# One 128x64 scan state for all heads: narrow state products, row-tiled inter products, one update per block, in a two-layer hybrid mixer

## The chip, the cores and the metric

The kernel runs on one core of one Trainium2 chip. The metric is the device time of one execution in microseconds; the time before is the median of three runs.

## The reference

Two layers act on 1024 latent tokens and 256 context tokens of width 1024. In each layer one input projection feeds three head groups: neighbourhood attention (8 heads), gated linear attention (GLA, 4 heads with keys of 32 and values of 64) and HGRN2 (4 heads with keys and values of 64). GLA and HGRN2 are scans in both directions, first over the context and then over the latents:

```python
def step(state, xs):
    q_i, k_i, v_i, d_i = xs
    o_i = jnp.einsum('bhcd,bhdv->bhcv', q_i, state)
    state = d_i[..., None] * state + jnp.einsum('bhcd,bhcv->bhdv', k_i, v_i)
    return state, o_i
```

`state` is a matrix of keys by values for each head. The output of a chunk is the inter part `o_i`, that reads the state, plus an intra part from the chunk's own tokens. The groups are gated, joined, and projected back with a residual.

## The kernel before

Activations lie with features on the 128 partitions and the 1280 tokens along the free axis, in SBUF buffers of 128x1280 fp32 (`big`, 34 of them). The dense products split an fp32 operand into a high and a low fp32r part and make three matmuls of it (`proj`, L306 to L308, PSUM tile pj); scans and attention multiply in plain fp32.

`scan_run` handles one scan: GLA with `nh=4` heads of `dk=32` keys (`hp = npair = 2` pairs of heads; names that end in g), HGRN2 with two heads of 64 keys at a time (`hp = npair = 1`; names that end in h). Per layer it runs once for GLA and twice for HGRN2, six times in all. The 128 partitions of keys hold all heads of a run, `dk` each. Tokens go in ten blocks of 128, two to a step, with steps 0 to 5 (step 5 has no new block pair) and then a backward loop `k = 2..5`. In a step:

- `prep` (of the next step) makes the decayed keys and queries on GpSimd, ScalarE and VectorE.
- `diag` (tile l, L598), `level` 0 to 2 (tile lv, L639) and `add_levels` (L662) build the intra matrix A of the two blocks. l and lv come from the PSUM pool `pss` (two buffers of two banks).
- `turn` (ktp, L670) transposes the decayed keys of the step before; `states` multiplies them with the values (pu, L682) and updates the forward state. pu and ktp come from `pst` (two buffers of one bank).
- `outs` makes the outputs of the step before: inter products with the state (L698) and intra products with A (L704) into po, which ScalarE copies out (L711).

The backward direction keeps its transposed keys in `ktb`: `back_states` (pub, L721) and `back_outs` (pi, L734, added to the output by VectorE in L742) run in step 5 and in the backward loop. In layer 1 the context blocks need no output.

The state of a run is a block-diagonal 128 x (64 nh) matrix: head h has its rows `h*dk` and its columns `64*h`, the rest is zero. So the state product of a block is one 128x128 product per pair of heads, whose off-diagonal part is thrown away, and `state_step` updates it head by head (L526 for the first block, L528 else: old state times decay plus product), nh VectorE instructions a block. The inter product contracts all 128 rows, against zeros for the other heads: 128 rows by 64 columns a head in `outs`, 128 by 128 a pair in `back_outs`. The forward states rotate through three places in zk, zz_ and ab[0], the backward ones through four in zk, which is cleared again in step 5 (L765).

TensorE and SyncE run in the order in which the program is written; the instructions of the other engines are ordered by a planner's simulated times, and PSUM and SBUF buffers are handed out by it too. Between the parts of a scan stand calls `fill(ns)`: each puts so many nanoseconds' worth of dense projections of later stages into TensorE's order, counted from a table and not from a clock. Wherever a tile of matmul operands is smaller than 128 rows or columns, several such matmuls use different parts of the array.

Of the kernel before, what the change touches and what calls it, by code (L numbers as in the profile page):

```python
# [12 lines left out]
F32 = mybir.dt.float32  # L13
# [6 lines left out]
P = 128  # L20
# [42 lines left out]
def hybrid_kernel(ctx: ExitStack, tc: tile.TileContext, a: dict, out: bass.AP):  # L63
# [424 lines left out]
    def scan_run(l, tag, nh, q, ks, G, dec, gs, vts, vgs, oTs, nxt=()):  # L488
# [5 lines left out]
        sw_ = npair * P  # L494
# [5 lines left out]
        nc.gpsimd.memset(zk, 0.0)  # L500
        nc.gpsimd.memset(zz_, 0.0)
        nc.gpsimd.memset(ab[0][:, 1024:], 0.0)
# [5 lines left out]
        spare = (zk, zz_, ab[0]) if hp == 2 else (zz_, zz_[:, P:], ab[0])  # L508
        Sf = [t[:, 1024:1024 + sw_] for t in spare]
        Sb = [zk[:, sw_ * i:sw_ * i + sw_] for i in range(4)]  # L510
# [165 lines left out]
        def states(e):  # L676
            pu = pst.tile([P, 512], F32, tag="t1", name="pu")
            js = [j for j in range(2) if 2 * e["step"] + j < 9]
            for j in js:
                for pr in range(npair):  # L680
                    c = j * sw_ + pr * P
                    nc.tensor.matmul(pu[:, c:c + P], e["kt"][:, j], vts[pr][:, 2 * e["step"] + j, :], start=True, stop=True)  # L682
            for j in js:
                s = 2 * e["step"] + j
                state_step(0, Sf[s % 3], Sf[(s + 1) % 3], s, s == 0, pu, j * sw_)

        def outs(e, pool, tg):
            if not e["intra"]:
                return
            po = pool.tile([P, 512] if tg == "t1" else [P, 1024], F32, tag=tg, name="po")  # L690
            col = lambda pr, j: slice(256 * pr + P * j, 256 * pr + P * j + P)
            for j in range(2):
                s = 2 * e["step"] + j
                A = e["A"][0] if hp == 1 else e["A"][j]
                for pr in range(npair):
                    for hb in range(2):
                        if s > 0:
# [5 lines left out]
                    for hb in range(2):  # L703
                        nc.tensor.matmul(  # L704
                            po[hb * 64:hb * 64 + 64, col(pr, j)], vts[pr][:, s, hb * 64:hb * 64 + 64],
                            A[:, 2 * hb + j if hp == 1 else 2 * pr + hb, :], start=(s == 0), stop=True,
                            skip_group_check=True,
                        )
            c0 = 256 * e["step"]
            for pr in range(npair):  # L710
                nc.scalar.copy(oTs[pr][:, c0:c0 + 256], po[:, 256 * pr:256 * pr + 256])  # L711
# [3 lines left out]
        def back_states(k):  # L715
            pu = pst.tile([P, 512], F32, tag="t1", name="pub")
            ns = [n for n in (2 * k, 2 * k + 1) if n < 9]
            for i, n in enumerate(ns):
                for pr in range(npair):
                    c = i * sw_ + pr * P  # L720
                    nc.tensor.matmul(pu[:, c:c + P], ktb[:, order[n], :], vts[pr][:, order[n], :], start=True, stop=True)  # L721
            for i, n in enumerate(ns):
                state_step(1, Sb[n % 4], Sb[(n + 1) % 4], order[n], n == 0, pu, i * sw_)

        def back_outs(k):
# [4 lines left out]
            for i, n in enumerate(ns):  # L730
                s = order[n]
                for pr in range(npair):
                    c = i * sw_ + pr * P
                    nc.tensor.matmul(  # L734
                        po[:, c:c + P], Sb[n % 4][:, pr * P:(pr + 1) * P], G[1][:, s * P:(s + 1) * P], start=True, stop=True
                    )
            for i, n in enumerate(ns):
                s = order[n]
                for pr in range(npair):
                    c = i * sw_ + pr * P  # L740
                    sl = oTs[pr][:, s * P:(s + 1) * P]
                    nc.vector.tensor_tensor(sl, po[:, c:c + P], sl, op=ALU.add)  # L742
# [5 lines left out]
        for step in range(6):  # L748
# [15 lines left out]
            if step == 5:  # L764
                nc.gpsimd.memset(zk[:, 0:4 * sw_], 0.0)  # L765
# [28 lines left out]
            if pe:  # L794
                outs(pe, *((pst, "t1") if step < 5 else (pss, "s2")))
# [659 lines left out]
```

## Time and profile before

| | us |
|---|---|
| median of 3 runs | 1872.86 (1872.14 to 1873.64) |
| the profiled execution | 1871.71 |
| its span | 1869.9 |
| TensorE (PE) busy | 1722.7 |
| VectorE (DVE) busy | 1069.9 |
| ScalarE (ACT) busy | 824.9 |
| GpSimd (POOL) busy | 495.9 |

A profile line names the source line, the engine, the operation, the tiles (out<-in) and their shape. A matmul's shape is given as rows*columns of the part of the array that it uses, and then the moving operand. A matmul's duration is its time from issue to end; matmuls overlap, so what a stream of them costs is read from one start to the next. PEld is the weight load that belongs to a matmul. A plain fp32 product appears as two matmul instructions.

### The profile page before, as it was taken

Reading aid. Unit: us, or ns where it says so; the run is one execution under the profiler, and the core shown is the slowest. Engines: PE = TensorE matmul, PEld = TensorE weight load, DVE = VectorE, ACT = ScalarE, POOL = GpSimd, SP = SyncE. Lnnn points to the kernel's source line nnn. Section 1 sums busy time; section 2 is a strip of 40 time slices with the busy share of each in tenths; the row PEclk is TensorE's granted clock in tenths of the full one; section 3 lists DMA queues with packets and bytes.
Section 4 is the critical chain, followed back from the end, with each engine's and each line's share of the span. In section 5 each row is a group of like instructions: output and inputs, shape, how many; then the busy total and the mean of one; then the engine's idle time right before and its main releaser. Section 6 shows DMA issues by size and latency. Waiting matters only on the chain. (4 is left out here: it accounts for less than half of the span.)

```text
span 1869.9 us, 33649 instructions
## 1 busy us (share of the span) xinstructions
PE 1722.7 (92%) x13392; PEld 1339.3 (72%) x13392; DVE 1069.9 (57%) x2304; ACT 824.9 (44%) x1869; POOL 495.9 (27%) x572
## 2 busy tenths in 40 slices
PE   4799998899999999998998998898999999998986
PEld 2567787777777777775786787786777777766765
DVE  4656977865634433344658688767645353334546
ACT  4344433544425544465424453354243364455533
POOL 2143432553520110111101564235324011011102
PEclk8799999899999999998999999999999999999998
DMA  9452131221320412144332012112213131244212
GB/s 340 162 194 87 56 104 52 75 80 51 108 72 29 138 54 100 49 146 140 128 126 88 23 52 94 60 63 91 68 55 117 48 117 45 108 135 155 74 66 90
DMA packets 78908, 179.50 MB, mean 96 GB/s; under 512 B 8896, under 2 KB 19392, under 8 KB 78752
## 3 DMA queue, kind: packets, MB, share of 16 engines
q1 hardware_dynamic: 44608, 100.93, 16.2%
q10 hardware_dynamic: 27936, 49.56, 7.4%
q0 software_dynamic: 6208, 26.87, 4.2%
q8 instruction: 105, 1.72, 0.4%
q14 instruction: 51, 0.42, 0.1%
HBM read 131.59 MB, written 45.74 MB: 95 GB/s over the span
## 5 line engine op out<-in xcount | busy, mean ns | idle before, releaser
L306 PE MATMUL pj<-hhi,whi 128*128 128x512 f32 (+1 forms) x1416 | 567.0, 400 | 21.9 <-DVE sg L412 11.2
L307 PE MATMUL pj<-hlo,whi 128*128 128x512 f32 (+1 forms) x1416 | 532.6, 376 | 0.0
L308 PE MATMUL pj<-hhi,wlo 128*128 128x512 f32 (+1 forms) x1416 | 531.8, 376 | 0.0
L306 PEld LDWEIGHTS pj<-hhi,whi 128*128 128x128 f32 x1416 | 273.0, 193 | 98.1 <-issue 27.4
L308 PEld LDWEIGHTS pj<-hhi,wlo 128*128 128x128 f32 x1416 | 273.1, 193 | 54.4 <-DVE wlo L283 0.2
L307 PEld LDWEIGHTS pj<-hlo,whi 128*128 128x128 f32 x1416 | 273.9, 193 | 42.9 <-issue 2.3
L283 POOL TENSOR_TENSOR wlo<-wst,whi 128x512 fp32r<-128x512 f32 x80 | 110.1, 1377 | 681.7 <-ACT whi L282 619.3
L1013 DVE CUSTOM_DVE_ANT_0 sp<-sps,tab 128x640 f32<-128x640 f32 (+2 forms) x144 | 102.6, 748 | 157.0 <-PE sps L1005 156.9
L1016 ACT ACTIVATE sp<-sp,mn 128x640 f32<-128x640 f32 (+2 forms) x144 | 110.2, 766 | 166.1 <-DVE mn L1013 159.3
L282 ACT CAST whi<-wst 128x512 fp32r<-128x512 f32 x144 | 83.5, 617 | 99.0 <-PE pj L307 74.6
L283 DVE TENSOR_TENSOR wlo<-wst,whi 128x512 fp32r<-128x512 f32 x64 | 55.1, 861 | 124.0 <-ACT whi L282 119.9
L1220 DVE SCALAR_TENSOR_TENSOR xn<-py,m,xn 128x512 f32<-128x512 f32 (+1 forms) x88 | 56.8, 650 | 73.8 <-PE py L1215 68.9
L1033 PE MATMUL ptp<-cst,sp 128*128 128x128 f32 x640 | 91.3, 274 | 8.3 <-ACT PT L1038 3.1
L1033 PEld LDWEIGHTS ptp<-cst,sp 128*128 128x128 f32 x640 | 76.2, 141 | 28.1 <-ACT PT L1038 4.4
L1005 PE MATMUL sps<-nk,nq 64*128 64x256 f32 (+1 forms) x544 | 89.6, 444 | 0.0
L1046 PE MATMUL pv<-PT,nv 128*64 128x128 f32 x1280 | 87.1, 281 | 2.0 <-ACT PT L1038 1.1
L324 ACT ACTIVATE sg<-pj 128x512 f32<-128x512 f32 (+1 forms) x90 | 47.9, 532 | 90.6 <-PE pj L308 85.8
L1046 PEld LDWEIGHTS pv<-PT,nv 128*64 128x64 f32 x1280 | 69.6, 138 | 18.9 <-issue 12.7
L1005 PEld LDWEIGHTS sps<-nk,nq 64*128 64x128 f32 x544 | 47.3, 188 | 38.4 <-issue 23.4
L1213 PE MATMUL py<-oh,whi 128*128 128x512 f32 (+1 forms) x160 | 65.9, 412 | 7.3 <-ACT whi L282 6.7
L1213 PE MATMUL py<-oh,wo 128*128 128x256 f32 (+1 forms) x192 | 67.9, 354 | 4.9 <-ACT wo L282 4.9
L1038 ACT COPY PT<-ptp 128x256 f32<-128x256 f32 (+1 forms) x120 | 58.6, 488 | 28.4 <-PE ptp L1033 27.9
(301 smaller groups left out, 3177.0 us busy)
## 6 DMA issues: line engine op xcount, KB each, us to landing
wst<-in_w_in SPq DMA_DIRECT2D x128, 256.0 KB, 3.1
adw<-in_ada_w SPq DMA_DIRECT2D x48, 512.0 KB, 7.4
pre<-sg ACTq DMA_DIRECT2D x80, 256.0 KB, 2.1
tab<-in_rpbt SPq DMA_DIRECT2D x16, 640.0 KB, 4.7
wst<-in_w_out SPq DMA_DIRECT2D x32, 256.0 KB, 3.4
oscr<-sg ACTq DMA_DIRECT2D x23, 256.0 KB, 2.2
hlf<-pre POOLq DMA_DIRECT2D x8, 640.0 KB, 4.7
nk<-pre POOLq DMA_DIRECT2D x8, 640.0 KB, 5.3
```

What stands on the lines that cost most here:

```text
L282: nc.scalar.copy(hi, st)
L283: (nc.vector, nc.gpsimd)[WPOOL[h]].tensor_tensor(lo, st, fence(hi), op=ALU.subtract)
L306: nc.tensor.matmul(ps[:, :n], hi[:, k, :], mv(hh[k]), start=(k == 0), stop=False)
L307: nc.tensor.matmul(ps[:, :n], hi[:, k, :], mv(hl[k]), start=False, stop=False)
L308: nc.tensor.matmul(ps[:, :n], lo[:, k, :], mv(hh[k]), start=False, stop=(k == KT - 1))
L1005: nc.tensor.matmul(sps[h][:, pc:pc + w], q[RG[h], qc:qc + P], k[RG[h], kc:kc + w], start=True, stop=True)
L1013: nc.vector.tensor_tensor_reduce(sp, sps[h][:, c0:c0 + n], tabs[h][:, tb:tb + n], -1.0, 3.0e38, ALU.add, ALU.min, mn)
L1016: nc.scalar.activation(sp, sp, AF.Exp, bias=mn, scale=-1.0, accum_out=sm)
L1033: nc.tensor.transpose(pt[:, c - lo:c - lo + P], st[i]["sp"][:, c:c + P], ident)
L1038: nc.scalar.copy(dst, src)
L1046: nc.tensor.matmul(pv[RG[h], 0:P], v3[:, c, RG[h]], st[i]["PT"][:, (h * len(chs) + j) * P:(h * len(chs) + j + 1) * P], start=(j == 0), sto ...
L1213: nc.tensor.matmul(ps[:, :n], w[0][:, k, :], mh, start=(k == ks[0]), stop=False)
```

## The change

All heads of a run share one state tile of 128x64: head h has its `dk` rows, the columns are the 64 values. The state products become one product per head, `dk` columns of the array by 64 moving columns (`state_mm`). `state_step` becomes one VectorE instruction a block, over 128 partitions. The inter products contract only the head's own `dk` rows: tiles of 32 rows by 64 columns for GLA, 64 by 64 for HGRN2; in `outs` all inter products of both blocks now come ahead of all intra products, and only the first product of a head clears its bank. po of GLA moves from `pst` to `pss`, pair pr in a bank of its own, and pi is laid out likewise. The forward states live in zz_, the backward ones in sh; the clearing of zk in step 5 and part of the clearing at a run's start are dropped.

```diff
-        nc.gpsimd.memset(zk, 0.0)
-        nc.gpsimd.memset(zz_, 0.0)
-        nc.gpsimd.memset(ab[0][:, 1024:], 0.0)
+        nc.gpsimd.memset(zk[:, 0:1024], 0.0)
+        nc.gpsimd.memset(zz_[:, 0:1024], 0.0)
...
-        spare = (zk, zz_, ab[0]) if hp == 2 else (zz_, zz_[:, P:], ab[0])
-        Sf = [t[:, 1024:1024 + sw_] for t in spare]
-        Sb = [zk[:, sw_ * i:sw_ * i + sw_] for i in range(4)]
+        Sf = [zz_[:, 1024 + 64 * i:1088 + 64 * i] for i in range(3)]
+        Sb = [sh[:, 1024 + 64 * i:1088 + 64 * i] for i in range(4)]
+        HR = [slice(h * dk, (h + 1) * dk) for h in range(nh)]
...
-        def state_step(d, old, new, s, first, up, c0):
+        def state_mm(pu, c0, kt, s):
             for h in range(nh):
-                rows = slice(h * dk, (h + 1) * dk)
-                c, cu = slice(h * 64, (h + 1) * 64), slice(c0 + h * 64, c0 + (h + 1) * 64)
-                if first:
-                    nc.vector.tensor_copy(new[rows, c], up[rows, cu])
-                else:
-                    nc.vector.scalar_tensor_tensor(
-                        new[rows, c], old[rows, c], dec[d][3][rows, s:s + 1], up[rows, cu], op0=ALU.mult, op1=ALU.add
-                    )
+                v = vts[h // 2][:, s, 64 * (h % 2):64 * (h % 2) + 64]
+                nc.tensor.matmul(pu[HR[h], c0:c0 + 64], kt[:, HR[h]], v, start=True, stop=True, skip_group_check=True)
+
+        def state_step(d, old, new, s, first, up):
+            if first:
+                nc.vector.tensor_copy(new, up)
+            else:
+                nc.vector.scalar_tensor_tensor(new, old, dec[d][3][:, s:s + 1], up, op0=ALU.mult, op1=ALU.add)
...
-                for pr in range(npair):
-                    c = j * sw_ + pr * P
-                    nc.tensor.matmul(pu[:, c:c + P], e["kt"][:, j], vts[pr][:, 2 * e["step"] + j, :], start=True, stop=True)
+                state_mm(pu, 64 * j, e["kt"][:, j], 2 * e["step"] + j)
...
-        def outs(e, pool, tg):
+        def outs(e, last):
...
-            po = pool.tile([P, 512] if tg == "t1" else [P, 1024], F32, tag=tg, name="po")
-            col = lambda pr, j: slice(256 * pr + P * j, 256 * pr + P * j + P)
+            if hp == 1 and not last:
+                po = pst.tile([P, 512], F32, tag="t1", name="po")
+            else:
+                po = pss.tile([P, 1024], F32, tag="s2", name="po")
+            col = lambda pr, j: slice(512 * pr + P * j, 512 * pr + P * j + P)
+            begun = set()
+            for j in range(2):
+                s = 2 * e["step"] + j
+                if s == 0:
+                    continue
+                for h in range(nh):
+                    pr, hb = h // 2, h % 2
+                    nc.tensor.matmul(
+                        po[RG[hb], col(pr, j)], Sf[s % 3][HR[h]], e["QE"][0][HR[h], j * P:(j + 1) * P],
+                        start=h not in begun, stop=False, skip_group_check=True,
+                    )
+                    begun.add(h)
...
-                            nc.tensor.matmul(
-                                po[hb * 64:hb * 64 + 64, col(pr, j)],
-                                Sf[s % 3][:, pr * P + hb * 64:pr * P + hb * 64 + 64],
-                                e["QE"][0][:, j * P:(j + 1) * P], start=True, stop=False, skip_group_check=True,
-                            )
...
-                    nc.tensor.matmul(pu[:, c:c + P], ktb[:, order[n], :], vts[pr][:, order[n], :], start=True, stop=True)
+                state_mm(pu, 64 * i, ktb[:, order[n], :], order[n])
...
-                for pr in range(npair):
-                    c = i * sw_ + pr * P
+                for h in range(nh):
+                    c = 512 * (h // 2) + P * i
                     nc.tensor.matmul(
-                        po[:, c:c + P], Sb[n % 4][:, pr * P:(pr + 1) * P], G[1][:, s * P:(s + 1) * P], start=True, stop=True
+                        po[RG[h % 2], c:c + P], Sb[n % 4][HR[h]], G[1][HR[h], s * P:(s + 1) * P], start=True, stop=True,
+                        skip_group_check=True,
                     )
...
-                nc.gpsimd.memset(zk[:, 0:4 * sw_], 0.0)
...
-                outs(pe, *((pst, "t1") if step < 5 else (pss, "s2")))
+                outs(pe, step == 5)
```

## Rows read from the trace of the kernel before

**Rows 1.** The page's part 1: busy us, share of the span, instructions.
```profile
PE 1722.7 (92%) x13392; PEld 1339.3 (72%) x13392; DVE 1069.9 (57%) x2304; ACT 824.9 (44%) x1869; POOL 495.9 (27%) x572
```
**Rows 2.** Stretches, first GLA scan: length, busy us per engine, clock, DMA share, GB/s.
```profile
188.00:312.00 124.00, 113.89 (x1200) 94.65 (x1199) 107.35 (x243) 46.62 (x120) 46.40 (x62) 0.97 0.20 69
```
**Rows 3.** Groups by shape: count, busy us, mean ns, idle before and its releaser.
```profile
L721 PE MATMUL pub<-vt,ktbg 128*128 128x128 f32 x72 | 11.6, 311 | 9.2 <-DVE zkg L528 9.2
L734 PE MATMUL pi<-hlf,zkh 128*128 128x128 f32 x68 | 11.3, 281 | 0.0
L734 PE MATMUL pi<-glf,zkg 128*128 128x128 f32 x68 | 10.5, 284 | 2.3 <-DVE zkg L528 2.3
L528 DVE SCALAR_TENSOR_TENSOR zkh<-zkh,e10h,pub 64x64 f32<-64x64 f32 x64 | 17.9, 280 | 22.1 <-PE pub L721 20.3
L528 DVE SCALAR_TENSOR_TENSOR zkg<-zkg,e10g,pub 32x64 f32<-32x64 f32 x64 | 17.7, 277 | 1.9
```
**Rows 4.** Timeline of PE, a backward turn of GLA: start us, length us, instruction.
```profile
299.83 0.39 PE L308 MATMUL pj<-hhi,wlo 128*128 128x512 f32 x1
300.06 1.05 PE L721 MATMUL pub<-vt,ktbg 128*128 128x128 f32 x8
300.95 1.06 PE L734 MATMUL pi<-glf,zkg 128*128 128x128 f32 x8
301.76 0.48 PE L306 MATMUL pj<-hhi,whi 128*128 128x512 f32 x1
302.07 0.40 PE L307 MATMUL pj<-hlo,whi 128*128 128x512 f32 x1
```
**Rows 5.** Timeline of PE, level 1 and states of GLA's step 1, and pj.
```profile
200.41 0.46 PE L639 MATMUL lv<-zg,swg 64*32 64x64 f32 x32
200.79 1.16 PE L682 MATMUL pu<-vt,swg 128*128 128x128 f32 x8
201.71 0.48 PE L306 MATMUL pj<-hhi,whi 128*128 128x512 f32 x1
```
**Rows 6.** Timeline, level 2 and outs of a GLA step, add_levels on DVE among them.
```profile
249.81 0.39 PE L308 MATMUL pj<-hhi,wlo 128*128 128x512 f32 x1
250.13 0.67 PE L639 MATMUL lv<-zg,swg 64*64 64x128 f32 x16
250.73 0.44 PE L698 MATMUL po<-swg,zzg 128*64 128x128 f32 x4
...
251.29 1.29 DVE L662 TENSOR_TENSOR abg<-lv,abg 128x512 f32<-128x512 f32 x2
...
252.31 0.39 PE L704 MATMUL po<-abg,vt 128*64 128x128 f32 x4
252.62 0.50 PE L306 MATMUL pj<-hhi,whi 128*128 128x512 f32 x1
252.96 0.39 PE L307 MATMUL pj<-hlo,whi 128*128 128x512 f32 x1
```
**Rows 7.** Waits of PE in the whole span: us in total, times, longest us.
```profile
PE pub L721 <- DVE zkg L528: 9.2, 2, 5.2
...
PE lv L639 <- DVE abg L662: 4.7, 1, 4.7
...
PE pi L734 <- DVE zkg L528: 2.3, 4, 1.2
...
PE po L698 <- DVE zzg L526: 1.8, 1, 1.8
```
**Rows 8.** Groups by shape: the modulation's column tiles.
```profile
L157 PE MATMUL adps<-adw,sil 128*32 128x512 f32 x192 | 27.5, 638 | 11.6 <-DMA adw<-in_ada_w 11.6
```
**Rows 9.** Timeline of DVE, the updates that PE's first wait for pub ends with.
```profile
284.17 0.97 DVE L526 COPY zkg<-pub 32x64 f32<-32x64 f32 x4
...
285.49 1.21 DVE L528 SCALAR_TENSOR_TENSOR zkg<-zkg,e10g,pub 32x64 f32<-32x64 f32 x4
```
**Rows 10.** Timeline of DVE in the GLA scan of layer 1, before lv's wait.
```profile
1123.78 1.21 DVE L528 SCALAR_TENSOR_TENSOR abg<-zzg,e10g,pu 32x64 f32<-32x64 f32 x4
```

More of the change, by code (lines that the diff above doesn't have):

```diff
@@ L493, in scan_run @@
         npair = hp = nh // 2
-        sw_ = npair * P
         full = l == 0
@@ L679, in states @@
             for j in js:
-                for pr in range(npair):
-                    c = j * sw_ + pr * P
-                    nc.tensor.matmul(pu[:, c:c + P], e["kt"][:, j], vts[pr][:, 2 * e["step"] + j, :], start=True, stop=True)
+                state_mm(pu, 64 * j, e["kt"][:, j], 2 * e["step"] + j)
             for j in js:
                 s = 2 * e["step"] + j
-                state_step(0, Sf[s % 3], Sf[(s + 1) % 3], s, s == 0, pu, j * sw_)
-        def outs(e, pool, tg):
+                state_step(0, Sf[s % 3], Sf[(s + 1) % 3], s, s == 0, pu[:, 64 * j:64 * j + 64])
+        def outs(e, last):
             if not e["intra"]:
                 return
-            po = pool.tile([P, 512] if tg == "t1" else [P, 1024], F32, tag=tg, name="po")
-            col = lambda pr, j: slice(256 * pr + P * j, 256 * pr + P * j + P)
+            if hp == 1 and not last:
[15 more added lines that the diff above has]
+                    begun.add(h)
             for j in range(2):
@@ L694, in outs @@
                 A = e["A"][0] if hp == 1 else e["A"][j]
-                for pr in range(npair):
-                    for hb in range(2):
-                        if s > 0:
-                            nc.tensor.matmul(
-                                po[hb * 64:hb * 64 + 64, col(pr, j)],
-                                Sf[s % 3][:, pr * P + hb * 64:pr * P + hb * 64 + 64],
-                                e["QE"][0][:, j * P:(j + 1) * P], start=True, stop=False, skip_group_check=True,
-                            )
[L703 to L708, printed above, removed]
+                for h in range(nh):
+                    pr, hb = h // 2, h % 2
+                    nc.tensor.matmul(
+                        po[RG[hb], col(pr, j)], vts[pr][:, s, hb * 64:hb * 64 + 64],
+                        A[:, 2 * hb + j if hp == 1 else 2 * pr + hb, :], start=h not in begun, stop=True,
+                        skip_group_check=True,
+                    )
+                    begun.add(h)
             c0 = 256 * e["step"]
             for pr in range(npair):
-                nc.scalar.copy(oTs[pr][:, c0:c0 + 256], po[:, 256 * pr:256 * pr + 256])
+                nc.scalar.copy(oTs[pr][:, c0:c0 + 256], po[:, 512 * pr:512 * pr + 256])
         order = [1, 0] + list(range(9, 1, -1))
@@ L718, in back_states @@
             for i, n in enumerate(ns):
-                for pr in range(npair):
-                    c = i * sw_ + pr * P
-                    nc.tensor.matmul(pu[:, c:c + P], ktb[:, order[n], :], vts[pr][:, order[n], :], start=True, stop=True)
+                state_mm(pu, 64 * i, ktb[:, order[n], :], order[n])
             for i, n in enumerate(ns):
-                state_step(1, Sb[n % 4], Sb[(n + 1) % 4], order[n], n == 0, pu, i * sw_)
+                state_step(1, Sb[n % 4], Sb[(n + 1) % 4], order[n], n == 0, pu[:, 64 * i:64 * i + 64])
         def back_outs(k):
@@ L731, in back_outs @@
                 s = order[n]
-                for pr in range(npair):
-                    c = i * sw_ + pr * P
+                for h in range(nh):
+                    c = 512 * (h // 2) + P * i
                     nc.tensor.matmul(
-                        po[:, c:c + P], Sb[n % 4][:, pr * P:(pr + 1) * P], G[1][:, s * P:(s + 1) * P], start=True, stop=True
+                        po[RG[h % 2], c:c + P], Sb[n % 4][HR[h]], G[1][HR[h], s * P:(s + 1) * P], start=True, stop=True,
+                        skip_group_check=True,
                     )
@@ L739, in back_outs @@
                 for pr in range(npair):
-                    c = i * sw_ + pr * P
+                    c = 512 * pr + P * i
                     sl = oTs[pr][:, s * P:(s + 1) * P]
```

## The prediction

> **What bounds the kernel now.** I read the page's part 1 first: TensorE (PE) is busy for 1722.7 of 1869.9 us, VectorE (DVE) for 1069.9 [rows 1]. So the time is PE's own stream of matmuls plus the moments in which it stands. The second view is the table of stretches, laid on the first GLA scan, because the average hides it: there DVE is busy for 107.35 of 124 us, next to PE's 113.89 [rows 2]. A scan is thus the one place where both engines matter. PE keeps its program order, and the order was fixed when the program was traced (the projections that fill it come in amounts counted from a table, not from the clock). A microsecond taken out of PE's stream is therefore a microsecond of the kernel, unless a later wait takes it back, and a shorter DVE queue pays only where PE waits for it. The third view, the groups by shape, gives the counts and durations of the edited lines [rows 3]; the timelines give what PE really pays, from start to start [rows 4 to 6]; the waits say where PE stands for the scan state [rows 7].
>
> **How a product is priced.** An fp32 product is two instructions ("passes"). There are 9 blocks in a direction and two layers, so the GLA scan with its two head pairs shows 9 x 2 x 2 x 2 = 72 backward state passes, HGRN's four scans with one pair each have as many [rows 3]. In [rows 4] 8 + 8 passes of 128x128 fill 300.06 to 301.76 us: 1.70 us, 15 steps of 0.11 and a last one of 0.03; a pass is 0.112 us. Narrow tiles run side by side: from 250.73 to 252.31 us are 28 passes of 128*64 in 1.58 us [rows 6], so two of them (a lot) take 0.109 us. The 16 passes of 64*64 tiles with 128 columns take 0.60 us up to the next line [rows 6] and the 32 passes of 64*32 tiles with 64 columns 0.38 us [rows 5]. With 0.15 us for leaving the shape, that is 4 lots of four at 0.11 us and 4 lots of eight at 0.056 us. So a lot costs what its columns cost, however many tiles share it. Column tiles of 128 rows by 32, which the new state products use, do the same: 192 passes of 638 ns lie in 27.5 us [rows 8], some four and a half deep.
>
> **Changing the tile shape costs too.** From one pj to the next is 0.23 us; from pj to a tiled line 0.32 [rows 6], and the first lot comes 0.05 late: 0.14 into tiles. From the last lots (252.31, 0.22 us of work) to pj is 0.31, and from that pj to the second 0.34 instead of 0.23 [rows 6]: 0.20 out of tiles. From tiles to other tiles I take 0.14, from [rows 6], and from tiles to 128*128 fp32 0.19, from 0.92 us for the 8 passes of pu [rows 5]. Between pj and 128*128 fp32 it is nothing: 0.23 in, and 0.31 instead of 0.23 after a last pass of 0.03 instead of 0.11 [rows 4].
>
> **State products, L682 and L721.** 36 GLA blocks (18 forward, 18 backward) go from 4 passes (0.448 us) to 2 lots of four (0.112): 12.1 us saved. 72 HGRN blocks go from 2 passes (0.224) to 2 lots of two (0.112): 8.1 us. The price of a 64-column lot is that of [rows 5]. The Trainium skill, TensorEngine Tiling (Array Packing), Instruction Overhead, speaks against narrowing an already small dimension: about 60 cycles of overhead for each matmul; as an estimate from that page 25 ns more a lot, which would leave 14.8 of the 20.2 us. The 0.056 us of [rows 5] show no such addition, and the sum goes by the row.
>
> **Inter products, L698 and L734.** 68 backward GLA passes are 17 blocks [rows 3], the forward ones the same 17. Forward, 4 lots of two (0.44 us) become 2 lots of four (0.22): 3.7 us. Backward, 4 passes (0.448) become 2 lots of four: 3.9 us. HGRN's 34 blocks each way stay at 2 lots or passes (0.22): nothing. No row has 32-row tiles; the nearest are the 64-row lots of [rows 6]. If only two of the four run side by side, 7.5 us of this go.
>
> So products give 20.2 + 7.6 = **27.8 us**.
>
> **New changes of shape.** Per scan: states in steps 1 to 4 now leave tiles for pj (4); step 5 has two entries and exits more around its state products and two more around outs and back_outs (6); the four last turns, that went through 128*128 without a change, get pj, state tiles, inter tiles, pj (3 x 3 and 2 without states): 11. That is 21, in six scans 126, and 7 more between inter and intra in GLA's outs, where HGRN's inter tiles share the 64*64 shape of the level before them: 133. By kind: 36 more into tiles at 0.14, 66 more out at 0.20, 61 more between tiles at 0.14, 30 fewer from tiles to 128*128 at 0.19: 5.0 + 13.2 + 8.5 - 5.7 = **21.0 us lost**. At 0.10 each they would be 13.3, at 0.20 26.6. PE's own gain is 6.8 us. All of it comes from GLA: a clean backward turn goes from 2.24 us [rows 4] to 0.23 + 0.14 + 4 x 0.056 + 0.14 + 4 x 0.109 + 0.20 + 0.23 = 1.60, while HGRN's goes from 0.23 + 8 x 0.112 + 0.23 = 1.36 up to the same 1.60.
>
> **State updates, L526 and L528.** Of 288 DVE instructions (36 blocks x 4, 72 x 2) 108 stay. 64 partitions take 280 ns where 32 take 277 [rows 3], so 128 should take 0.28, and 180 x 0.278 = 50 us of DVE go. What PE gets of it: **(a)** PE waits twice, 9.2 us in all, for pub's PSUM buffer [rows 7]. The buffer comes free after 0.97 + 1.21 us of updates [rows 9], in the new kernel after 0.24 + 0.28: 1.7 us sooner each, 3.4 us; what is late then is DVE's queue ahead of them. **(b)** The 2.3 us before pi [rows 7] are waits for one block's four updates, and go: 2.3. **(c)** The 4.7 us before lv [rows 7] wait for add_levels; in the DVE queue ahead of it stand eight such updates (the second four: [rows 10]): 1.7. **(d)** The 1.8 us before po [rows 7] end with the first of four copies, but the intra products of the other block, which ran meanwhile, now come behind: 0.3. Sum 7.7. Where PE waits on the gates and the forget filler of a DVE that is 87% busy [rows 2], I take 2 more, out of 0 to 6: an estimate, one part in 25 of the 50 us.
>
> **PSUM and memsets.** GLA's po moves from pst to pss, where l0 and lv live. In [rows 7] lv is what waits for add_levels, not the l issued before it, so buffers go by which is free, and po gets l0's, idle since its copy. The next l then takes whichever of po's and lv's comes free first; the projections between hide that, and without them it costs up to the 1.29 us of add_levels [rows 6], with ScalarE's copies and all of PE's stream queued behind. I take nothing. The dropped memsets are GpSimd's, which is busy for 495.9 us [rows 1], and no PE wait names one: nothing. Sb in sh instead of zk has the same life.
>
> **The sum.** 6.8 + 7.7 + 2 = 16.5 us off the profiled execution's 1871.7 (a span of 1869.9 and 1.8 around it) gives 1855.2. The median of the runs is 1.15 us above that execution: **1856**.
>
> **Rivals.** *1, slower: tiles on different rows that share a PSUM bank run one after the other.* po and pi now put heads 0 and 1, rows 0 to 31 and 32 to 63 (HGRN: 0 to 63 and 64 to 127), into one bank, at different partitions. In the kernel before row tiles always write banks of their own (r * 512), so no row decides it. HGRN's 68 inter blocks would pay 0.44 instead of 0.22, 15.0 us, and GLA's 34 another 7.5: 1856 + 22.5 = **1878.5**. It turns slower once 73% of that is serial. The Trainium skill states this as a rule (TensorEngine Tiling (Array Packing), Gotcha 1: PSUM Pressure: different row tiles cannot access the same bank simultaneously). Against it: the partitions differ, and column tiles share a bank in [rows 8] without a delay. 0.12. *2: the waits stay.* DVE's order is planned anew, and other work moves ahead of the updates; only PE's 6.8 us are left: **1866**. For it: in (a) DVE was behind with other work by itself. 0.18. *3: po gets lv's buffer* and waits for add_levels; in [rows 6] po starts at 250.73 and add_levels ends at 252.58. Seven times 1.85 is 13: **1870**. 0.10. The forecast has 0.60.
>
> **Range and chances.** Best: shape changes at 0.10 (7.7 less) and all 18.0 us of state waits gone: 1838. With the unknown 32-row tiles and changes at 0.20 the forecast's mechanism ends at 1869. 1843 to 1873 leaves out rival 1 and the best corner. A measurement here can tell some 0.2%, 3.7 us. Faster: 0.59 of the forecast, 0.13 of rival 2, 0.04 of rival 3: 0.76. Slower: 0.10 of rival 1 and 0.02: 0.12. Same: 0.12.
>
> **What would show it.** Right: pu and pub of GLA as 16 short passes in about a quarter of the time; pi and po lots of four starting some 7 ns apart; 108 updates of 128x64 near 280 ns; a GLA turn near 1.6 us, HGRN's longer than before; pub's waits 1.7 us shorter. Wrong: inter lots 0.2 us apart in pairs (rival 1), PE waits on DVE unchanged in sum (rival 2), po waiting for abg L662 (rival 3), or shape changes that cost other than 0.14 to 0.20 us.

## The result, and the profile after

The changed kernel takes 1850.5 us in the median (1848.5 to 1851.6, four runs), the kernel before 1872.5 us (1869.1 to 1873.6) in the same comparison: a ratio of 0.9885 with an interval of 0.9872 to 0.9899. That is 22 us less; 16.5 were forecast. The profiled execution took 1850.2 us, its span is 1848.4.

The page's part 1 of the changed kernel (busy us, share of the span, instructions), against [rows 1]:

```profile
PE 1711.9 (93%) x13816; PEld 1305.8 (71%) x13816; DVE 1010.7 (55%) x2124; ACT 824.4 (45%) x1869; POOL 487.8 (26%) x560
```

PE is busy for 10.8 us less and idle for 10.7 us less (147.2 to 136.5 of the span); DVE has lost 180 instructions and 59 us, 50 of them forecast. The groups by shape (count, busy us, mean ns, idle before and its releaser) show the new forms, against [rows 3]:

```profile
L522 PE MATMUL pub<-vt,ktbg 128*32 128x64 f32 x144 | 4.2, 227 | 4.8 <-DVE e20h L482 2.7 <-DVE e40h L482 2.1
L737 PE MATMUL pi<-hlf,shh 64*64 64x128 f32 x136 | 11.8, 284 | 0.0
L737 PE MATMUL pi<-glf,shg 32*64 32x128 f32 x136 | 6.0, 282 | 0.0
L528 DVE SCALAR_TENSOR_TENSOR shg<-shg,e10g,pub 128x64 f32<-128x64 f32 x16 | 4.4, 276 | 1.1 <-PE pub L522 0.9
```

144 narrow passes of GLA's backward states lie in 4.2 us where 72 wide ones lay in 11.6. HGRN's backward inter products (136 in 11.8) have gained nothing, as forecast. An update of 128 partitions lasts 276 ns, where one of 32 lasted 277.

A backward turn of GLA in PE's timeline (start us, length us, instruction), against [rows 4]:

```profile
289.26 0.39 PE L308 MATMUL pj<-hhi,wlo 128*128 128x512 f32 x1
289.58 0.43 PE L522 MATMUL pub<-vt,ktbg 128*32 128x64 f32 x16
289.94 0.67 PE L737 MATMUL pi<-glf,shg 32*64 32x128 f32 x16
290.54 0.50 PE L306 MATMUL pj<-hhi,whi 128*128 128x512 f32 x1
290.88 0.40 PE L307 MATMUL pj<-hlo,whi 128*128 128x512 f32 x1
```

From 289.26 to 290.88 us it takes 1.62 us, where 1.60 were forecast and 2.24 stood before. The waits of PE (us in total, times, longest), against [rows 7]:

```profile
PE pj L306 <- DVE sg L412: 12.0, 4, 3.9
...
PE pub L522 <- DVE e10h L482: 2.9, 1, 2.9
PE pub L522 <- DVE e20h L482: 2.7, 1, 2.7
...
PE pub L522 <- DVE e40h L482: 2.1, 1, 2.1
...
PE lv L637 <- DVE abg L660: 1.5, 2, 1.2
...
PE l L596 <- DVE abg L660: 1.4, 1, 1.4
```

There is no row any more for pi on an update, nor for po on GLA's first copy. The pub rows name an operation of the next scan's preparation (L482), because DVE ran it right behind the update that frees the buffer: at GLA's first wait the update runs from 275.24 to 275.51 us, e40h from 275.43 to 275.62, and pub starts at 275.66. The rows of e40h and e20h are GLA's (4.8 us), the row of e10h is the first HGRN scan's.

**Where the time went.** The table of stretches, laid on the six scans of each kernel, from a scan's first diagonal product to its last backward inter product (length, busy us of PE, PEld, DVE, ACT and POOL, clock, DMA share, GB/s). Before:

```profile
170.00:313.30 143.30, 133.19 (x1433) 111.05 (x1433) 125.18 (x274) 55.24 (x139) 55.68 (x72) 0.98 0.19 64
323.90:444.60 120.70, 111.24 (x1232) 90.34 (x1232) 86.72 (x195) 56.31 (x141) 58.47 (x74) 0.96 0.22 70
456.10:567.10 111.00, 108.81 (x1213) 85.90 (x1213) 61.58 (x147) 38.41 (x98) 39.04 (x56) 1.00 0.23 78
1102.80:1227.90 125.10, 113.52 (x1172) 94.76 (x1172) 105.34 (x236) 44.10 (x110) 52.04 (x67) 0.95 0.21 70
1251.20:1354.70 103.50, 92.88 (x988) 74.51 (x988) 73.46 (x154) 39.73 (x99) 48.68 (x69) 0.93 0.24 80
1379.50:1476.20 96.70, 92.78 (x990) 72.93 (x990) 49.05 (x119) 27.98 (x72) 33.68 (x47) 0.96 0.26 90
```

After:

```profile
164.60:295.70 131.10, 125.10 (x1540) 99.71 (x1539) 107.78 (x225) 55.54 (x142) 54.71 (x70) 0.99 0.22 72
306.60:429.40 122.80, 113.41 (x1286) 88.67 (x1285) 84.96 (x177) 57.69 (x146) 54.43 (x72) 0.94 0.21 69
441.10:554.90 113.80, 110.07 (x1266) 83.70 (x1266) 56.99 (x129) 39.80 (x103) 39.60 (x57) 0.99 0.23 77
1090.80:1206.20 115.40, 107.96 (x1276) 84.79 (x1275) 87.38 (x187) 44.50 (x111) 49.34 (x63) 0.96 0.23 77
1229.80:1332.70 102.90, 94.45 (x1040) 72.55 (x1040) 63.97 (x136) 40.14 (x99) 46.01 (x67) 0.93 0.24 81
1357.60:1454.70 97.10, 93.18 (x1042) 69.85 (x1041) 43.45 (x100) 28.18 (x72) 32.99 (x46) 0.98 0.26 89
```

The first and fourth rows are GLA: 268.4 us become 246.5, 21.9 less. PE's busy time gives 13.7 of it (246.7 to 233.1), its idle time 8.3 (21.7 to 13.4). The other four are HGRN: 431.9 become 436.6, 4.7 **more**, nearly all in PE's busy time (405.7 to 411.1). The remaining 5.4 us lie ahead of the first scan (it begins at 170.0 and at 164.6). PE's 688 matmuls there are the same in all kernels, but the order of the other engines' work is not. 3.7 of the 5.4 us lie in the last 88 of these matmuls (17.3 us before, 13.6 after), at a wait that the kernel before has and the changed one has not. The waits of PE at adtp, small products of the modulation, before and in e5 (below; us in total, times, longest):

```profile
PE adtp L162 <- ACT sg L193: 2.0, 1, 2.0
```

```profile
PE adtp L162 <- ACT sg L193: 1.9, 1, 1.9
```

ScalarE's copy sg stands there behind a cast (L282) that waits 2.71 us for a transfer of weights, 0.58 us after the change. Behind PE's wait the projection matmuls of 256 columns follow each other after 0.21 us instead of 0.12, at half the granted clock. It is no chance of one execution: those 88 matmuls take 17.1 to 17.3 us in all four profiles of kernels that keep the old memsets in GLA's scans (before, e2, e4, e5), 16.3 to 16.4 in e1 and e6 to e8, and 13.6 to 13.7 in the other six. The other 1.7 us lie earlier and differ from profile to profile.

The lengths of most kernels below (us; profiled executions, split in the same way; "rest" is what lies between and behind the scans, up to the last matmul):

| kernel | median | ahead | GLA | HGRN | rest |
|---|---|---|---|---|---|
| before | 1872.5 | 170.0 | 268.4 | 431.9 | 988.1 |
| after | 1850.5 | 164.6 | 246.5 | 436.6 | 989.2 |
| e1, updates per head | 1885.2 | 168.6 | 265.3 | 451.9 | 988.8 |
| e2, narrow products alone | 1877.7 | 169.7 | 266.4 | 440.3 | 988.6 |
| e3, GLA alone | 1849.0 | 165.9 | 246.3 | 431.2 | 989.7 |
| e4, HGRN alone | 1878.2 | 169.9 | 270.4 | 435.1 | 991.4 |
| e5, memsets back | 1847.2 | 170.0 | 246.2 | 430.3 | 988.5 |
| e11, interleaved | 1854.5 | 165.8 | 247.4 | 443.0 | 990.3 |
| e12, longer chain | 1864.9 | 166.7 | 252.9 | 442.6 | 989.4 |

### The profile page after: what moved, and what is told of

It reads as the page before. It is cut to its first block, busy times and chain, and to the rows that moved or that the text cites. A ratio compares the mean times of both kernels' runs of the same rounds, so it can differ in the third digit from the quotient of the medians.

```text
span 1848.4 us, 34314 instructions
## 1 busy us (share of the span) xinstructions
PE 1711.9 (93%) x13816; PEld 1305.8 (71%) x13816; DVE 1010.7 (55%) x2124; ACT 824.4 (45%) x1869; POOL 487.8 (26%) x560
## 5 line engine op out<-in xcount | busy, mean ns | idle before, releaser
L1019 ACT ACTIVATE sp<-sp,mn 128x640 f32<-128x640 f32 (+2 forms) x144 | 110.1, 766 | 165.9 <-DVE mn L1016 159.1
L282 ACT CAST whi<-wst 128x512 fp32r<-128x512 f32 x144 | 83.7, 617 | 109.1 <-PE pj L307 83.4
L283 DVE TENSOR_TENSOR wlo<-wst,whi 128x512 fp32r<-128x512 f32 x64 | 49.5, 774 | 131.9 <-ACT whi L282 128.1
L1049 PEld LDWEIGHTS pv<-PT,nv 128*64 128x64 f32 x1280 | 69.7, 138 | 18.8 <-issue 12.7
```

Source lines behind the costliest of these rows:

```text
L282: nc.scalar.copy(hi, st)
L283: (nc.vector, nc.gpsimd)[WPOOL[h]].tensor_tensor(lo, st, fence(hi), op=ALU.subtract)
L1019: nc.scalar.activation(sp, sp, AF.Exp, bias=mn, scale=-1.0, accum_out=sm)
L1049: nc.tensor.matmul(pv[RG[h], 0:P], v3[:, c, RG[h]], st[i]["PT"][:, (h * len(chs) + j) * P:(h * len(chs) + j + 1) * P], start=(j == 0), sto ...
```

## The experiments

The theory under test is the prediction's: PE's own products give some 7 us and the shorter chain of updates some 8, two terms that add up. The rivals: PE's stream alone explains it, or the updates alone do, or the two depend on each other.

**e1: the updates per head again, the rest as after.**

```diff
-            if first:
-                nc.vector.tensor_copy(new, up)
+            for r in HR:
+                if first:
+                    nc.vector.tensor_copy(new[r], up[r])
...
```

> The changed kernel with its one state update per block undone alone: each head's rows are updated by an operation of their own again (4 per block in GLA, 2 in HGRN), TensorE's stream stays as it is after. If the waits of TensorE on the state updates were the larger part of the gain (they shrank by some 9 us between the two traces, against 6.8 us of shorter products), those waits come back and the time is about 1860 us (1857 to 1865). If TensorE's shorter work explains it alone, the time stays at 1850 to 1853 us.

Measured: 1885.2 us (1881.6 to 1887.9), ratio to before 1.0066, interval 1.0051 to 1.0081. Both expectations are missed: it is 35 us over the changed kernel and slower than the kernel before. PE runs the same 13816 instructions as after. The stretches of the two GLA scans and the first HGRN scan (columns as above):

```profile
168.60:311.20 142.60, 132.37 (x1540) 104.50 (x1539) 126.53 (x280) 56.47 (x143) 54.62 (x70) 0.95 0.20 65
322.10:455.50 133.40, 118.02 (x1286) 92.31 (x1285) 91.36 (x195) 57.82 (x146) 56.26 (x72) 0.90 0.20 63
...
1118.70:1241.40 122.70, 110.72 (x1276) 86.20 (x1275) 102.40 (x237) 44.10 (x110) 51.63 (x66) 0.94 0.22 71
```

The counts of matmuls, 1540, 1286 and 1276, are those of after. In GLA PE stands 22.2 us where it stood 13.4, and its identical instructions are busy for 243.1 us where they took 233.1. So with an update per head GLA's scans take 265.3 us: of the 21.9 us that the change took off them, 18.8 are back. Over all six scans the waits grew by 17 us and the busy time by 17; 2.7 us more lie ahead of the first scan, in the 88 matmuls named above. The waits on the updates:

```profile
PE pub L522 <- DVE shg L529: 9.2, 2, 5.0
...
PE pub L522 <- DVE shh L529: 4.8, 1, 4.8
...
PE pi L740 <- DVE shg L529: 1.7, 4, 0.7
```

GLA's pub rows are back at the 9.2 us of [rows 7], and HGRN has one of 4.8 that stands in neither other kernel at that length (0.35 before at that place, 2.9 after). Most of the added busy time is the clock's. The stretches before, behind and after that 4.8 us wait:

```profile
420.00:428.00 8.00, 7.83 (x38) 5.41 (x37) 8.00 (x8) 3.00 (x8) 5.81 (x7) 1.00 0.31 89
430.70:437.60 6.90, 4.00 (x16) 3.21 (x17) 5.84 (x22) 2.45 (x8) 1.21 (x3) 0.51 0.10 38
438.00:446.00 8.00, 8.00 (x71) 6.13 (x70) 2.00 (x7) 2.01 (x4) 1.29 (x1) 1.00 0.13 29
```

The granted clock is 1.00, then 0.51, then 1.00: PE had been busy at 2.4 GHz, stood for the wait, and then ran at 1.2 GHz. In that stretch one pj of 512 columns follows another after 0.43 us, elsewhere after 0.23. The means over the whole span say how much of this there is:

```profile
core 0: 1869.9 us, clock 0.962
core 0: 1848.4 us, clock 0.965
core 0: 1886.1 us, clock 0.956
```

These are before, after and e1. With levels of 1 and 0.5 they mean 2 x 0.038 x 1869.9 = 142 us at 1.2 GHz before, 129 after and 166 in e1: 37 more than after, whose work takes up to half of that, 18 us, longer. So a wait is paid twice here: by its length, and by the work behind it. (e12 shows below that it need not be.)

**e2: narrow state products alone.** Block-diagonal states, updates per head and wide inter products stay as before.

```diff
-                for pr in range(npair):
-                    c = i * sw_ + pr * P
-                    nc.tensor.matmul(pu[:, c:c + P], ktb[:, order[n], :], vts[pr][:, order[n], :], start=True, stop=True)
+                state_mm(pu, i * sw_, ktb[:, order[n], :], order[n])
```

> The kernel before with the state products alone made narrow (per head 128 rows x 32 or 64 columns of the array, 64 values wide); states stay block-diagonal, one update per head, inter products in full 128-row tiles. By the prices of the prediction the products give 20.2 us and the added changes of tile shape take about 14 (some 24 forward bursts at 0.15, some 30 backward at 0.34), so about 1866 us (1862 to 1870), with the waits on the updates still there. If the updates were no part of the gain, it comes near the changed kernel, 1851 to 1856 us. If a change of tile shape costs nothing here, 1852 us too, but then with the waits of before in the trace.

Measured: 1877.7 us (1871.8 to 1880.4), ratio 1.0026, interval 1.0015 to 1.0037: slower than before, and none of the three cases. The some 6 us that the prices promise are in the trace: the stretches that hold state products, from the projection matmul before them to the second one behind, take 6.0 us less in sum without their idle time (GLA's 8.7 less, HGRN's 2.7 more). They are eaten by waits (pub 9.7 and 2.5, lv on add_levels 6.1 us) and by a clock of 0.958, 158 us at 1.2 GHz. The sum of the six stretches of e2 (length, busy us by engine):

```profile
sum 706.70, PE 652.87 PEld 516.47 DVE 503.47 ACT 261.65 POOL 286.05; mean PE 108.81 PEld 86.08 DVE 83.91 ACT 43.61 POOL 47.68
```

PE is busy in them for as long as before (652.4) and stands for 53.8 us instead of 47.9. Over 4022 steps in which one projection matmul follows another directly, the same before, after, in e1 and in e2, the time goes from 921.4 before to 931.8 us (935.0 in e1, 925.2 after). Making PE's products shorter without making DVE's chain shorter turned the gain into waiting and slow clock here. That e2 came out slower than before, and not the same, can't be laid on the chain alone: GLA's scans are 2.0 us shorter than before and HGRN's 8.4 longer, 5.2 of them in the first HGRN scan (125.9 us, 120.7 before), and there a wait has another cause as well.

It is the wait of 2.5 us for pub. GpSimd and DVE in the first HGRN scan of e2 (timeline, start us, length us, instruction, idle time before it):

```profile
417.17 0.59 POOL L357 DMA_DIRECT2D hv<-pre  x1 [2.48 <-DMA pre<-sg]
417.76 1.19 POOL L500 MEMSET zkh<- 128x1280 f32 x1
418.87 1.18 POOL L501 MEMSET zzh<- 128x1280 f32 x1
```

```profile
417.29 3.05 DVE L945 TENSOR_SCALAR hk<-hlf 128x512 f32<-128x512 f32 x1
```

And the same operation after the change:

```profile
394.99 0.42 DVE L945 TENSOR_SCALAR hk<-hlf 128x512 f32<-128x512 f32 x1
```

It lasts 3.05 us instead of 0.42, until 0.3 us past the end of the memsets; behind it stand 7 us of DVE's preparation of the next scan and then the copy that frees pub's buffer. In e1 it lasted 2.61, beside the same three instructions of GpSimd, the first of which had begun 0.1 us before it both times. The Trainium skill, SBUF — State Buffer, SBUF: two separate sides, has a rule for such a pair: GpSimd and VectorE's operations in a two-port mode need the same pair of SBUF ports, and whichever starts first holds it for its whole instruction, while the other is blocked. The trace agrees in that GpSimd was first and that the operation ends just behind the memsets; it stood through three instructions of GpSimd, not one, and no run here shows in which mode the operation ran. In the kernel before, such an operation had ended 1.2 us ahead of the memsets; after the change it began 0.1 us ahead of GpSimd's DMA (395.10) and ended 0.3 us ahead of the memsets: that is luck of the order.

**e3 and e4: the change in GLA's scans alone, and in HGRN's alone.** Each caller takes its own version of the scan:

```diff
-        scan_run(l, "h", 2, u["q"], u["ks"], u["G"], u["dec"], 1.0, [vt], [vg], [oT], nxt)
+        scan_run_old(l, "h", 2, u["q"], u["ks"], u["G"], u["dec"], 1.0, [vt], [vg], [oT], nxt)
```

(e3; in e4 the call for "g" instead.)

> The change in the GLA scans alone, HGRN's scans as before. HGRN's bursts after show 0.24 us more for each row-tiled inter product burst and nothing won in its products, so I expect the whole gain to be GLA's: 1849 us (1846 to 1853), no slower than the changed kernel. If HGRN's updates (two per block before, one after) carry a third of the gain, it is 1856 to 1860 us.

> The change in the HGRN scans alone, GLA's as before: the other side of the split. Expected 1872 us (1868 to 1876), no gain, if what its DVE saves is what its changes of tile shape cost; 1863 to 1866 us if HGRN carries a third of the gain.

Measured: e3 1849.0 us (1846.5 to 1850.6), ratio 0.9876, interval 0.9861 to 0.9890; e4 1878.2 us (1875.8 to 1880.1), ratio 1.0033, interval 1.0020 to 1.0046. GLA alone brings the whole gain (its scans 246.3 us, after 246.5). HGRN alone is 6 us slower than before, past the range expected. In its profile the four HGRN scans took 3.2 us more than before, the unchanged GLA scans 2.0 and the rest 3.3, so less than half of the loss is seen where the change is.

**e5: the dropped memsets put back.**

```diff
-        nc.gpsimd.memset(zk[:, 0:1024], 0.0)
-        nc.gpsimd.memset(zz_[:, 0:1024], 0.0)
+        nc.gpsimd.memset(zk, 0.0)
+        nc.gpsimd.memset(zz_, 0.0)
+        nc.gpsimd.memset(ab[0][:, 1024:], 0.0)
...
+                nc.gpsimd.memset(zk[:, 0:512 * hp], 0.0)
```

> The changed kernel with the memsets that the change dropped put back: both full 1280 columns, the 256-column one, and the one of the backward states at step 5. The prediction costed their loss at nothing. If that holds: 1850 to 1853 us. Rival: GpSimd's longer memsets hold up VectorE (with narrow products and old updates one hk operation of VectorE lasted 3.05 us instead of 0.42 while GpSimd ran them), TensorE then waits at the backward turn and its clock falls behind the wait: 1854 to 1862 us, with the first HGRN scan longer than its 122.8 us.

Measured: 1847.2 us (1844.0 to 1848.6), ratio 0.9862, interval 0.9847 to 0.9877. In sum nothing is lost, but the memsets were not free everywhere: two things cancel. Ahead of the first scan the wait for ScalarE's copy is back (1.9 us, 3.7 with the slower work behind it). And with another order of the other engines' work HGRN's scans take 430.3 us instead of 436.6, with the same TensorE program: a wait of lv for GpSimd of 1.65 us at 1300 us after the change is not there in e5, nor is the first HGRN scan's wait of 2.9 us for pub. So up to 6 us of HGRN's time hang on the order that the planner happens to give, as much as e2 and e4 are slower than the kernel before; the two weren't separated further.

**e11: inter and intra products block by block, instead of all inter products of a burst first.**

```diff
             for j in range(2):
                 s = 2 * e["step"] + j
-                if s == 0:
-                    continue
+                A = e["A"][0] if hp == 1 else e["A"][j]
...
-            for j in range(2):
-                s = 2 * e["step"] + j
-                A = e["A"][0] if hp == 1 else e["A"][j]
                 for h in range(nh):
```

> The changed kernel with the forward inter and intra products of a block next to each other again, block by block, where the change puts all inter products of a burst ahead of all intra products: two more changes of tile shape in each of some 27 bursts, 54 in all. By the prediction's 0.14 us from tile to tile this costs 7.6 us: 1858 us (1855 to 1861). If grouping was free to leave out (a change of shape costs nothing by itself): 1850 to 1852 us.

Measured: 1854.5 us (1853.6 to 1859.8), ratio 0.9908, interval 0.9893 to 0.9922: 4 us over the changed kernel, under the range expected. PE's timeline shows the price itself:

```profile
245.38 0.45 PE L699 MATMUL po<-swg,zzg 32*64 32x128 f32 x8
245.76 0.66 PE L706 MATMUL po<-abg,vt 128*64 128x128 f32 x8
246.35 0.45 PE L699 MATMUL po<-swg,zzg 32*64 32x128 f32 x8
246.72 0.66 PE L706 MATMUL po<-abg,vt 128*64 128x128 f32 x8
247.31 0.50 PE L306 MATMUL pj<-hhi,whi 128*128 128x512 f32 x1
```

From 245.38 to 247.31 are 1.93 us; the same 32 products after the change, grouped, take 1.62 (243.85 to 245.47). Two changes of shape more cost 0.31 us, 0.155 each, against 0.14 in the sum. The 27 stretches that hold such bursts, from the projection matmul before them to the second one behind, grew by 8.4 us between the two profiles (7.6 expected); the profiled execution, the slowest of the four, took 9.6 us more. Where the others got half of that back isn't shown.

**e9, e10 and e12: a longer chain, put in on purpose.** Idle DVE operations behind the first backward product of each scan, in e9 three and in e10 six of 0.69 us on a free tile, in e12 eight of some 0.25 us on the state itself, between its copy and the update that needs it. e9 and e12:

```diff
+            for _ in range(3 if k == 0 else 0):
+                nc.vector.tensor_tensor(zk[:, 0:512], zk[:, 0:512], zk[:, 0:512], op=ALU.max)
```

```diff
+                for _ in range(8 if n == 0 else 0):
+                    nc.vector.tensor_tensor(Sb[1], Sb[1], Sb[1], op=ALU.max)
```

> The changed kernel with three idle VectorE operations (128x512, 0.68 us each, 2.05 together) put ahead of the first backward update of each of the six scans: a known wait added at one place. In three scans TensorE waits there already (2.09, 2.86 and 2.70 us at the backward state product), in three it does not. If a wait costs its own length: 6 to 8 us, 1857 to 1859 us. If TensorE's clock falls behind the longer wait and the work after it takes twice its time for a while, as the granted clock of the traces suggests, 1.7 to 3.4 us more for each scan in which it falls: 1862 to 1868 us, and the scans show more time at 1.2 GHz. If the place is covered by other work: 1850 to 1853 us.

> The same with six such operations, 4.1 us. Length alone: 12 us in the three scans that wait already and up to 6 in the others, 1863 to 1868 us. With the clock: 1870 to 1880 us. Covered: 1850 to 1854 us.

> The changed kernel with eight idle VectorE operations on the first backward state itself (128x64, some 0.25 us each, 2 us together), between its copy out of PSUM and the update that needs it, so that unlike the idle operations on a free tile they can't run ahead. It puts 2 us of the kind that the change removed (a longer update chain) back at one place in each of the six scans. If a longer chain costs its own length where TensorE waits on it: 2 us in each of GLA's two scans and the first HGRN scan, which wait there already, and up to 2 in the others: 6 to 12 us, 1857 to 1863 us. If the wait also takes TensorE's clock down, the scans show more time at 1.2 GHz and it is 1864 to 1872 us. If it is covered by the projections beside it: 1850 to 1853 us.

Measured: e9 1857.7 us (1854.2 to 1861.1, ratio 0.9927), e10 1858.0 us (1853.3 to 1862.2, ratio 0.9926). They tell little of the waits they were made for. The planner moved the operations ahead, since they touch only a free tile (a view of their tile in e10: count, duration, first and last start):

```profile
L726 DVE TENSOR_TENSOR zkg<-zkg x12: 673/691/1668, 251.8 to 1170.1; 128x512 f32<-128x512 f32 x12
```

The first runs at 251.8 us, while pub's copy comes at 275.5, and that wait is 2.09 us as after. GLA's first scan is unchanged (131.2 us in both, 131.1 after). The first HGRN scan's wait for pub went from 2.9 to 4.1 us, in e9 and e10 alike. HGRN's scans took 442.9 us in e9, where GpSimd's keys (swh) waited 2.7 us for an idle operation in DVE's queue and lv 4.70 us for GpSimd. Why six operations cost no more than three is open.

In e12 they stay in place: 1864.9 us (1863.0 to 1871.0), ratio 0.9969, interval 0.9960 to 0.9978, 14.4 us over the changed kernel, by its number at the lower end of the case in which the clock falls too. The waits:

```profile
PE pub L522 <- DVE zzg L528: 9.7, 2, 5.0
PE pub L522 <- DVE zzh L528: 5.8, 2, 4.2
```

GLA's two are 4.9 us longer (9.7 after 4.8), HGRN's 2.9 (5.8 after 2.9, a second one new). The idle time grew by 5.2 us in GLA and 6.0 in HGRN. In the third scan a new wait of 1.60 us came with a clock of 0.96 for the scan instead of 0.99, and the scan is 4.8 us longer. But the sum of the six stretches says that the clock had little part in the whole:

```profile
sum 695.50, PE 645.32 PEld 500.45 DVE 455.67 ACT 265.25 POOL 278.18; mean PE 107.55 PEld 83.41 DVE 75.94 ACT 44.21 POOL 46.36
```

The scans are 12.4 us longer than after the change (683.1). PE's idle time is 11.2 of it and its busy time 1.2 (644.2 to 645.3), and the 4022 projection steps took 927.6 us, 2.4 more. So here the longer chain cost its waits, nearly once.

**e6, e7 and e8: fewer and larger bursts.** In e6 the backward state products of blocks n = 2 to 8 join the last forward ones in one 512-column tile, and the backward loop holds none; the backward states get ten places in zk:

```diff
+            back = range(2, 9) if e["step"] == 4 else ()
+            for n in back:
+                state_mm(pu, 64 * n - 64, ktb[:, order[n], :], order[n])
...
+            for n in back:
+                state_step(1, Sb[n], Sb[n + 1], order[n], False, pu[:, 64 * n - 64:64 * n])
```

e7 also gathers the backward inter products into three bursts a scan, with one addition per burst and pair:

```diff
-            ns = [n for n in (2 * k + 1, 2 * k + 2) if n < 10 and (full or order[n] > 1)]
+            ns = {0: (1, 2), 1: (6, 5, 4, 3), 3: (9, 8, 7)}.get(k, ())
+            ns = [n for n in ns if full or order[n] > 1]
```

e8 does the same for GLA and leaves HGRN as before the change.

> The changed kernel with the backward state products of blocks n = 2 to 8 in one burst with the last forward one (one 512-column tile), so no state product in the backward loop: 18 changes of tile shape fewer at 0.14 us, and three waits of the backward turn for a free tile (2.9, 2.7 and 2.1 us in the trace after) have no place any more. Expected 1844 us (1840 to 1848). Rival: seven updates in a row (2 us of VectorE) hold up the operations behind them and TensorE waits at the inter products instead: 1850 to 1855 us.

> As the kernel with merged backward states, and the backward inter products in three bursts per scan where there were five, each added to the output in one operation per 128 rows: two bursts fewer at 0.34 us in six scans, and fewer VectorE operations. Expected 4 us under the kernel with merged states alone, about 1840 us (1836 to 1845); the same as that kernel if the added outputs come too late for the gates that read them.

> GLA's scans as in the kernel with merged states and inter products, HGRN's as before the change. HGRN's four scans together took 431.8 us before, 436.6 after and 431.1 where they were left as before, so this should be 1843 us (1839 to 1847), some 5 us under the changed kernel, if GLA alone carries the gain; if merging makes HGRN's share a gain too, the kernel with both merged is the faster of the two by 3 us or more.

Measured: e6 1850.1 us (1845.3 to 1854.6, ratio 0.9881): no gain. The waits of pub are gone, and others stand in their place, before GLA's outputs (2.04 and 2.63 us). In e7 they are still there:

```profile
PE po L703 <- DVE zzg L528: 4.7, 2, 2.6
```

PE comes to the outputs of GLA's last step 3 to 4 us sooner, counted from the scan's start, and waits there for the forward update, behind the same DVE queue. e7: 1841.5 us (1837.5 to 1848.3), ratio 0.9841, interval 0.9821 to 0.9861, the fastest here, 9 us under the changed kernel; e8: 1844.8 us (1843.3 to 1848.6), ratio 0.9858, interval 0.9844 to 0.9871. The two can't be told apart. e7 has 40 DVE instructions less than e6 (2084 and 2124) and 8 us less of PE's busy time (1701.9 and 1710.1): it shortened both engines' work, e6 only moved DVE's. In e7's first two HGRN scans the granted clock is 1.00 throughout, after the change it was 0.94 and 0.99.

## Why the prediction was right, and where it was not

**Products and shapes: right.** The order of tile shapes in PE's trace changes 555 times before and 688 times after, the 133 of the sum. A change costs 0.155 us (e11) against 0.14. GLA's turn takes 1.62 us (1.60). HGRN's turns of two blocks went from 1.42 to 1.69 us, by 0.27; the forecast had 1.36 and 1.60. The stretches that hold state, inter or output products, from the projection matmul before them to the second one behind, take 6.6 us less in sum without their idle time (GLA's 12.9 less, HGRN's 6.3 more), against 6.8. Rival 1 is refuted: the four 32-row tiles of a lot, two to a bank, start 7 ns apart and a lot takes 0.11 us; HGRN's two 64-row tiles share a bank as well and start 6 to 7 ns apart. The Trainium skill, TensorEngine Tiling (Array Packing), Gotcha 1: PSUM Pressure, says that different row tiles cannot access one bank at the same time; the measurement decides, for tiles that write different partitions of it.

**Waits for the state, forecast 7.7.** (a) pub, 3.4: GLA's 9.2 us became 4.8, 4.4 less, but HGRN's first scan got a wait of 2.9 where it had 0.35; net 1.9. What is left there is DVE's queue ahead of the copies, 6.87 us of the next scan's preparation before GLA's first, named but not priced; HGRN's wait isn't there in e5. (b) pi, 2.3: gone, as said. (c) lv, 1.7: 4.7 became 1.5, and 1.4 came back at the next l; this is the buffer wait of the moved po, taken as nothing with a bound of 1.29. Net 1.8. (d) po, 0.3: the whole 1.8. Sum 7.8. The sum agrees better than its terms: that is luck.

**The 2 us elsewhere: not there.** The wait of pj for DVE's gates (sg) went from 11.2 to 12.0 us, and lv's for GpSimd from 3.9 to 7.0; of the waits here named only that of pj for ScalarE's sg fell, from 5.6 to 3.6.

**The memsets and the stretch ahead: in no term.** The prediction put the dropped memsets at nothing, because no wait of PE names one. The wait for ScalarE's copy ahead of the first scan names none either, but it went with the change and came back with the memsets in e5: 3.7 us of the gain that no term foresaw.

**HGRN: the sign was in the text, the size not.** The sum had it in the added shape changes alone. It lost 4.7 us; e4 confirms a loss, e5 shows that up to 6 us there hang on GpSimd's order. Over the scans alone the change brought 17.2 us in the profile (21.9 less 4.7), against 16.5, out of a GLA better and an HGRN worse than the sum; the other 5.4 us lie ahead of them. For the medians, which differ by 22, the share of that stretch isn't known.

**What failed is that the terms were added.** The sum gave PE's 6.8 us a life of its own, and rival 2 (the waits stay) ended at 1866. e1 is that rival made real, e2 comes near it with the state products alone, and they took 1885 and 1878 us. In e1 a shorter stream ran into the same chain of updates earlier, waited longer, and then worked at 1.2 GHz. The prediction had no term for the clock, though [rows 2] show 0.97 for the first scan. Between before and after the clock moved little (0.962 to 0.965), so the forecast stood. For e1 the same sum, without what the single update gives, would have missed by 19 us and on the wrong side of 1872.

Open: what of e1's 35 us belongs to GpSimd's instructions beside DVE's (2.61 us for one operation, in a scan that is 10.6 us longer) and what to the chain; GLA's 18.8 us are not touched by that. Why e10 costs no more than e9. And what the single update gives by itself: no run has it together with the wide products, so it isn't shown that the narrow products were needed for the gain.

## What to carry to other kernels

When PE is the bound but waits in places for a chain on another engine, shorten that chain first or together with PE's part: shorter state products alone gained nothing here. Price a wait by its length, and take into the range that the work behind it may run at half the clock: in e1 that cost about as much as the waits, in e12 hardly anything. Look for the granted clock of the stretch, not of the span. Any edit also gives the other engines a new order, which moved several us here that no line of the edit names. Count changes of tile shape at 0.15 to 0.2 us each and gather bursts of one shape; a narrow tile that leaves its lot's columns as they are (HGRN's inter products) pays only these.

## What the runs showed of the hardware

- Two row tiles that write one PSUM bank at different partitions run side by side (two of 64 rows, or four of 32 rows in two banks): starts 7 ns apart, a lot of 128 columns 0.11 us. A 64-column lot of four column tiles takes 0.056 us.
- A change of tile shape between tiles costs 0.155 us.
- Behind a wait of 4.8 us the granted clock was 0.51 for 6.9 us, and a pj took 0.43 us a step instead of 0.23 (e1); behind one of 1.96 us, 256 columns took 0.21 us a step instead of 0.12 (before). The same TensorE program (13816 matmuls) was busy for 1711.9 and for 1731.8 us.
- An fp32 tensor-scalar operation of DVE, 0.42 us, lasted 3.05 (e2) and 2.61 us (e1) while GpSimd issued a DMA and ran two memsets.
